# Two of four weight-block sums of a unit made by accumulating transfers, adaLN sums spread over the gate/up and down stages, h kept in blocks of halves

## The chip, the cores and the metric

The kernel runs on one core of a Trainium2 chip. The metric is the device time in microseconds of one execution; the time given for a kernel is the median of its runs. The program computes in fp32: a product of matrices is made as three matmuls of fp32r operands, each operand being split into a rounded part (hi) and the rest (lo).

## The reference

Batch 1, 512 tokens, D = 1024, two layers, each a token mixer and a SwiGLU FFN of width 2816. Every sub-layer is wrapped in RMS norms and in adaLN: shift, scale and gate come from a conditioning vector c.

```python
def ada_modulation(c, w, b):
    m = jax.nn.silu(c) @ w + b
    shift, scale, gate = jnp.split(m, 3, axis=-1)
...
for i in range(DEPTH):
    shift, scale, gate = ada_modulation(c, mix_ada_w[i], mix_ada_b[i])
    h = rms_norm(x, mix_pre_g[i]) * (1.0 + scale) + shift
    y = stick_breaking_mixer(...) if i % 2 == 0 else token_mixing_mixer(...)
    x = x + gate * rms_norm(y, mix_post_g[i])
    shift, scale, gate = ada_modulation(c, ffn_ada_w[i], ffn_ada_b[i])
    h = rms_norm(x, ffn_pre_g[i]) * (1.0 + scale) + shift
    y = (jax.nn.silu(h @ w_gate) * (h @ w_up)) @ w_down
    x = x + gate * rms_norm(y, ffn_post_g[i])
```

The token-mixing mixer (gMLP) makes u and v = gelu(h @ w_in), takes the layer norm of v, mixes it over 128 positions with w_s (sv), and projects u * sv with w_out.

## The kernel before, in words

The stages follow each other: attention of layer 0 (stage 0), its output projection, FFN 0 (stage 1: gate/up, then down), the gMLP (stage 2), its output projection, FFN 1 (stage 3: gate/up, then down). Tokens lie in four tiles of 128 (`tt`), the contraction in blocks of 128 (`k`), the FFN width in 22 units of 128 (`f`).

*Engines.* Matmuls are recorded at L71, in the order in which the program writes them; the engines work each through its own list in order. Weights arrive by SP's queue in 512 KB slabs (`raw`), ACT makes their hi (L94) and DVE their lo (L95). `wget` emits the loads and splits of slabs ahead of their use, three by default and one for the sevens. SP's queue is one list too, so an issue that waits for a buffer holds those behind it.

*Gate/up.* The first three units are plain products (`unit`, names `gu`). The other 19 of each FFN are `seven` (names `r`): gate and up over two halves of the tokens and two halves of the contraction are a 2x2 by 2x2 block product, made with seven products instead of eight (Winograd's form). A seven is 7 × 4 × 3 = 84 matmuls of 256 columns. It needs sums of the activation blocks (`S`, made once at the boundary by `sums`) and sums of the weight blocks, made by `blocks` for every unit: from the two slabs x (halves B11, B22) and y (B21, B12), `f13` = x + B12 (L152, both halves in one DVE instruction), then `f24` in two additions (L161, L162). x, f13, f24 and the half B21 are split into hi and lo. Buffers: two `raw` for x, two `raw2` for y, shared with the adaLN slabs, two `f13`, one `f24`.

*adaLN sums.* The first pair of vectors (stage 0's pre-norm) is made in the attention by `ada0_sum`. The others are ten vectors of 1024, each a sum over eight slabs of 512 KB (`rawada`, L290) scaled by silu(c), on DVE (L265), then summed over partitions by two pairs of matmuls with ones (`adaps`, L306 to L308), for which the sum is split first (`acch`, `accl`, L303). They are a generator `Bg`, and a call of `bg.step(n)` issues n slabs or closing steps. G of a stage is the gate and the post-norm's weight; A and B are the scale and shift of the next stage. `Bg(0)` runs in the attention and stage 0's projection; `Bg(1)` (G, A, B, 24 slabs) in FFN 0's down projection, two per `k`; `Bg(2)` (24 slabs) in the gMLP while v is made, three per `k`; `Bg(3)` (G, 8 slabs) in FFN 1's down projection.

*Projections.* `out_proj` adds over `k` into eight banks (four token tiles, two halves). While adaLN steps run it lends the banks of one tile to `adaps`, keeps that tile's first part in `yp`, and adds the two parts at the end (L476). The last four `k` are the tail, token tile by token tile, so that `boundary` of a tile (norm, gate, residual, norm, transposes `tp`, split into `hTh`, `hTl`) runs beside the matmuls of the next ones. `hT` is kept as four pairs of tiles, each for two `k` and all 512 tokens; `boundary` splits a transposed bank in two halves (L374 to L379). All such tiles are slots of one pool, `s4`, with 27 buffers.

*gMLP.* Five u units of the first token half run in FFN 0's boundaries; then their second half, v in two column halves, u units 5 to 7 as matmuls of 512 columns, and `mix` (sv). The layer norm of v runs on DVE and ACT beside u units 5 to 7.

Of the kernel before, what the change touches and what calls it, by code (L numbers as in the profile page):

```python
# [13 lines left out]
P = 128  # L14
T = 512
# [11 lines left out]
def trunk(ctx: ExitStack, tc: tile.TileContext, A: dict, out: bass.AP):  # L27
# [5 lines left out]
    adas = ctx.enter_context(tc.tile_pool(name="adas", bufs=2))  # L33
    npool = ctx.enter_context(tc.tile_pool(name="npool", bufs=2))
    small = ctx.enter_context(tc.tile_pool(name="small", bufs=4))
    s4 = ctx.enter_context(tc.tile_pool(name="s4", bufs=27))
# [68 lines left out]
    def wload():  # L105

        src, a, b, _ = stream[len(raws)]
        if src is None:
            raws.append(None)
            return  # L110
        raw = wraw.tile([P, a, b], F32, tag="raw", name=nm("raw"))
        load(raw[:], src)
        raws.append(raw)

    def wemit():
# [4 lines left out]
        if src is None:  # L120
            got.append(blocks(*key[1:]))
            return
# [13 lines left out]
    def blocks(src):  # L136
# [5 lines left out]
        xr = wraw.tile([P, KD, P], F32, tag="raw", name=nm("rawb"))  # L142
        yr = fwork["raw"].tile([P, KD, P], F32, tag="raw2", name=nm("rawb"))
        for e, t in enumerate((xr, yr)):
            load(t[:], A[src[0]][src[1:] + (e,)])
# [4 lines left out]
        split(b21[0][:], b21[1][:], yr[:, 0:4, :])  # L150
        f13 = fp.tile([P, KD, P], F32, tag="f13", name=nm("f13"))
        dve.tensor_tensor(  # L152
            f13[:].rearrange("p (a k) f -> p a (k f)", a=2),
            xr[:].rearrange("p (a k) f -> p a (k f)", a=2),
            yr[:, 4:8, :].rearrange("p (a k) f -> p a (k f)", a=1).to_broadcast([P, 2, 512]),
            ALU.add,
        )
# [4 lines left out]
        dve.tensor_tensor(f24[:, 4:8, :], f24[:, 0:4, :], yr[:, 0:4, :], ALU.add)  # L162
# [40 lines left out]
    for l in range(2):  # L203
# [3 lines left out]
        for f in range(NH, KF):  # L207
            stream.append((None, 0, 0, ("blocks", ("wgu", l, f))))
# [59 lines left out]

    class Bg:
# [5 lines left out]
        def __init__(self, s):  # L275
            self.s = s
            self.parts = [("G", s, 2)]
            if s < 3:
                self.parts += [("A", s + 1, 1), ("B", s + 1, 0)]
            self.gen = self.run()  # L280

        def run(self):
            for name, s, part in self.parts:
                acc = slot(F32, name, 1, D)[:, 0, :]
                setattr(self, name, acc)
# [7 lines left out]
            for name, s, part in self.parts:  # L293
                acc = getattr(self, name)
# [47 lines left out]
    def boundary(s, tt, y, bg, xin, hT, S, tag):  # L342
# [4 lines left out]
        for hf, c in enumerate(halves):  # L347
# [3 lines left out]
            dve.tensor_tensor(t[:, c], y[hf][:], bg.G[:, c], ALU.mult)  # L351
# [13 lines left out]
        dve.tensor_tensor(t[:], x[:], bg.A[:], ALU.mult)  # L365
        dve.reciprocal(r1[:], sd[:])
        dve.scalar_tensor_tensor(t[:], t[:], r1[:, 0:1], bg.B[:], ALU.mult, ALU.add)
        late = []
        for q in range(2):
# [4 lines left out]
            for k2 in range(2):  # L374
                th, tl = hT[q * 2 + k2]
                src = ps[:, k2 * 256 : (k2 + 1) * 256].rearrange("p (a b) -> p a b", a=2)
                split(
                    th[:, :, tt * P : (tt + 1) * P], tl[:, :, tt * P : (tt + 1) * P], src
                )  # L379
            a = ps[:].rearrange("p (a b) -> p a b", a=4)  # L380
            if S is not None and tt < 2:
# [38 lines left out]
    def out_proj(s, nk, get_act, wkey, J, bg, hT, nxt=(), pre=None, S=None, steps=0):  # L420
# [6 lines left out]
        mid = -(-8 * len(bg.parts) // steps) + 1 if steps else None  # L427
# [20 lines left out]
        for k in range(nk - J):  # L448
# [5 lines left out]
            bg.step(steps)  # L454
            if k + 1 == mid:
# [9 lines left out]
        if hT is not None and not hT:  # L465
            hT.extend(new_hT())
# [3 lines left out]
        for tt in range(NT):  # L470
# [7 lines left out]
            if tt < 2:  # L478
                boundary(s, tt, y[tt], bg, xin, hT, S, "p" if last == 0 else "b")
                xs[tt + 2] = x_load(tt + 2)  # L480
        evacs, late = [], []
        for n, tt in enumerate((2, 3)):
            if nxt:
                evacs.append(nxt[n]())
            late.append(boundary(s, tt, y[tt], bg, xin, hT, S, "p" if tt == 3 else "b"))
# [14 lines left out]
    bg = Bg(0)  # L500
# [46 lines left out]
    def ada0_sum(raws, n, nk):  # L547
        acc = adas.tile([P, 512], F32, tag="acch", name=nm("acc"))
# [67 lines left out]
    for b in range(1, 4):  # L616
# [11 lines left out]
        if b < 3:  # L628
            wload()
            acc = ada0_sum(an, 512, 2)  # L630
# [245 lines left out]
    class Ffn:  # L876
# [10 lines left out]
        def unit(self, f, lo, n, look=3):  # L887

            w = self.w(f, look)
            if n == T:  # L890
                g, u = bank("g"), bank("u")
                gp, up = g[:], u[:]
            else:
                g = bank("gu")
                gp, up = g[:, :n], g[:, n:]
            for pb, ww in ((gp, w[0]), (up, w[1])):
                for k in range(KD):
                    h, l = hTk(self.hT, k, lo, n)
# [16 lines left out]
        def seven(self, f):  # L915
# [4 lines left out]
            W = wget(("blocks", ("wgu", self.li, f)), 1)  # L920
            R1, R2, R3 = [bank(n)[:, :256] for n in ("r1", "r2", "r3")]
            S = {n: (lambda k, t=self.S[n]: (t[0][:, k, :], t[1][:, k, :])) for n in "1234"}
            S["A11"] = lambda k: hTk(self.hT, k, 0, 256)
            S["A12"] = lambda k: hTk(self.hT, k + 4, 0, 256)
            S["A22"] = lambda k: hTk(self.hT, k + 4, 256, 256)
# [65 lines left out]
    STEPS = 3  # L991
# [8 lines left out]
    def gmlp(bg, hT, nhT, nS, nxt):  # L1000
# [13 lines left out]
        def v_mm(vb, tt, k, w):  # L1014
            a, b = hTk(hT, k, tt * P, P)
# [100 lines left out]
    )  # L1116
    f0.run(
        Bg(1), hT2,
# [101 lines left out]
```

## Time and profile before

| | us |
|---|---|
| three runs | 1215.77, 1218.69, 1218.76 |
| median | 1218.69 |
| profiled execution | 1216.18 |
| its span, first to last instruction | 1214.4 |
| around the span | 1.8 |

In the profile, PE is the matrix engine, PEld its weight loads, DVE the vector engine, ACT the scalar engine, POOL the general one; SPq, POOLq and so on are their queues of issues. The page gives each engine's busy share, the span in 40 slices of 30.4 us (digits are tenths; PEclk is the clock granted to the matrix engine), the chain of work that ended last, groups of instructions by line and tile, and DMA issues with their time from issue to landing. "out<-in" are the program's names of tiles. Where matmuls follow closely their recorded durations overlap, so a rate is taken from a stretch and its count. A few records of matmuls can be missing.

### The profile page before, as it was taken

Reading aid. Unit: us, or ns where it says so; the run is one execution under the profiler, and the core shown is the slowest. Engines: PE = TensorE matmul, PEld = TensorE weight load, DVE = VectorE, ACT = ScalarE, POOL = GpSimd, SP = SyncE. Lnnn points to the kernel's source line nnn. Section 1 sums busy time; section 2 is a strip of 40 time slices with the busy share of each in tenths; the row PEclk is TensorE's granted clock in tenths of the full one; section 3 lists DMA queues with packets and bytes.
Section 4 is the critical chain, followed back from the end, with each engine's and each line's share of the span. In section 5 each row is a group of like instructions: output and inputs, shape, how many; then the busy total and the mean of one; then the engine's idle time right before and its main releaser. Section 6 shows DMA issues by size and latency. Waiting matters only on the chain.

```text
span 1214.4 us, 18534 instructions
## 1 busy us (share of the span) xinstructions
PE 1179.5 (97%) x7336; PEld 1032.4 (85%) x7336; DVE 888.3 (73%) x1247; ACT 627.4 (52%) x1097; POOL 18.0 (1%) x30
## 2 busy tenths in 40 slices
PE   7898999999999999999999999899999999999998
PEld 4777778787899999998877898688999999998886
DVE  5878887766699888878763867785998888778224
ACT  6455766786555555556232542444655555555212
POOL 0100000000000000000000010000000000000000
PEclk9999999999999999999999999889999999999999
DMA  9666351120443333336883468734323333356311
GB/s 334 229 202 206 115 157 55 36 86 8 140 149 105 105 105 104 105 105 210 277 290 108 152 214 279 226 119 139 123 88 105 105 105 105 109 197 201 118 52 69
DMA packets 48634, 174.14 MB, mean 143 GB/s; under 512 B 5658, under 2 KB 5786, under 8 KB 48548
## 3 DMA queue, kind: packets, MB, share of 16 engines
q1 hardware_dynamic: 46820, 166.67, 42.8%
q0 software_dynamic: 1728, 6.29, 1.4%
q8 instruction: 57, 0.93, 0.3%
q14 instruction: 29, 0.24, 0.1%
HBM read 164.56 MB, written 8.39 MB: 142 GB/s over the span
## 4 chain that ended last, share of the span: by engine, by line
PE 71%; DMA 11%; DVE 11%; ACT 3%; issue 3%; SPq 0%; DVEq 0%; ACTq 0%
PE r L71 31%; PE y L71 20%; DMA rawada<-in_ada 6%; PE pqk L71 4%; PE gu L71 3%; PE av L71 2%; PE v L71 2%; DVE wl L95 2%; PE z3h L71 2%; PE z0h L71 2%; DMA raw<-in_wdown 2%; DVE A L265 1%; DMA raw<-in_win_v 1%; PE u L71 1%; ACT wh L94 1%
## 5 line engine op out<-in xcount | busy, mean ns | idle before, releaser
L71 PE MATMUL y<-wh,as 128*128 128x512 f32 x832 | 265.3, 397 | 0.0
L94 ACT ACTIVATE wh<-raw 128x1024 fp32r<-128x1024 f32 x112 | 118.4, 1059 | 208.8 <-PE y L71 105.9
L95 DVE TENSOR_TENSOR wl<-raw,wh 128x1024 fp32r<-128x1024 f32 x112 | 136.4, 1221 | 101.9 <-ACT wh L94 101.6
L71 PEld LDWEIGHTS y<-wh,as 128*128 128x128 f32 x832 | 157.3, 189 | 37.5 <-ACT B L310 0.4
L71 PE MATMUL r<-Sh,wh 128*128 128x256 f32 x608 | 170.1, 280 | 0.2 <-ACT e L938 0.2
L71 PE MATMUL r<-Sh,wl 128*128 128x256 f32 x608 | 170.3, 280 | 0.0
L71 PE MATMUL r<-Sl,wh 128*128 128x256 f32 x608 | 170.0, 280 | 0.0
L71 PE MATMUL y<-wl,as 128*128 128x512 f32 x416 | 165.1, 397 | 0.0
L95 DVE TENSOR_TENSOR wl<-f,wh 128x1024 fp32r<-128x1024 f32 x76 | 92.9, 1222 | 53.6 <-ACT wh L94 53.6
L94 ACT ACTIVATE wh<-f 128x1024 fp32r<-128x1024 f32 x76 | 80.7, 1061 | 76.1 <-PE r L71 72.3
L71 PEld LDWEIGHTS r<-Sh,wh 128*128 128x128 f32 x608 | 114.6, 189 | 0.4 <-ACT e L938 0.4
L71 PEld LDWEIGHTS r<-Sl,wh 128*128 128x128 f32 x608 | 114.5, 188 | 0.0
L71 PEld LDWEIGHTS r<-Sh,wl 128*128 128x128 f32 x608 | 114.5, 188 | 0.0
L71 PEld LDWEIGHTS y<-wl,as 128*128 128x128 f32 x416 | 78.7, 189 | 17.9
L71 PE MATMUL r<-hTh,wh 128*128 128x256 f32 x304 | 89.0, 293 | 0.0
L71 PE MATMUL r<-hTl,wh 128*128 128x256 f32 x304 | 84.9, 279 | 0.0
L71 PE MATMUL r<-hTh,wl 128*128 128x256 f32 x304 | 79.5, 280 | 0.0
L71 PEld LDWEIGHTS r<-hTh,wh 128*128 128x128 f32 x304 | 57.2, 188 | 5.4 <-DVE gu L948 0.7
L71 PE MATMUL r<-hTh,b 128*128 128x256 f32 x304 | 60.6, 282 | 0.0
L94 ACT ACTIVATE wh<-rawb 128x1024 fp32r<-128x1024 f32 x38 | 40.4, 1062 | 35.0 <-PE r L71 30.9
L71 PEld LDWEIGHTS r<-hTl,wh 128*128 128x128 f32 x304 | 57.3, 189 | 0.0
L95 DVE TENSOR_TENSOR wl<-rawb,wh 128x1024 fp32r<-128x1024 f32 x38 | 46.6, 1225 | 12.0 <-ACT wh L94 12.0
(245 smaller groups left out, 2664.1 us busy)
## 6 DMA issues: line engine op xcount, KB each, us to landing
rawada<-in_ada SPq DMA_DIRECT2D x80, 512.0 KB, 4.3
rawb<-in_wgu SPq DMA_DIRECT2D x76, 512.0 KB, 4.3
raw<-in_wdown SPq DMA_DIRECT2D x44, 512.0 KB, 4.2
raw<-in_wqk SPq DMA_DIRECT2D x16, 512.0 KB, 3.7
ada<-in_ada0p SPq DMA_DIRECT2D x12, 512.0 KB, 9.3
raw<-in_wgu SPq DMA_DIRECT2D x12, 512.0 KB, 4.4
xd<-x POOLq DMA_DIRECT2D x12, 512.0 KB, 2.9
x<-xd SPq DMA_DIRECT2D x12, 512.0 KB, 4.5
```

Source lines behind the costliest of these rows:

```text
L71: b = nc.tensor.matmul(o, l, r, start=start, stop=stop, skip_group_check=True)
L94: act.activation(hi, src, AF.Copy)
L95: dve.tensor_tensor(lo, src, hi.bitcast(F32), ALU.subtract)
L265: dve.scalar_tensor_tensor(acc, w, sc[:, kk : kk + 1], acc, ALU.mult, ALU.add)
```

## The change

- `blocks`: the second weight array `wy` holds, beside B21, the half B12 twice. f13 is loaded with x a second time, and POOL's queue adds the 512 KB `wy[4:12]` onto it by a transfer with `accum_op=add`; the DVE addition L152 is gone. y is loaded as 256 KB instead of 512. The transfers of a block are emitted one block ahead (`block_loads`). f24 is made as before.
- adaLN sums: G of stage 1 and A of boundary 1 in FFN 0's sevens (one or two steps a unit); B of boundary 1 and G of stage 2, then A and B of boundary 2, in FFN 0's down projection; in the gMLP what is left of the generator, one step per `k`; G of stage 3 in FFN 1's sevens, and no steps in FFN 1's down projection, so that there is no `yp` there. `adas` has one buffer of each kind instead of two, and the attention's sums take the two kinds in turn.
- hT: tiles of four `k` and 256 tokens, allocated as `boundary` comes to them; one split per transposed bank instead of two. Every matmul over `hT` has at most 256 columns; u units 5 to 7 take two where they took one. `s4` has 28 buffers.

The diff, without empty lines and most of its context; left out are the attention's and v's calls with the new names:

```diff
@@ -30,10 +30,10 @@
-    adas = ctx.enter_context(tc.tile_pool(name="adas", bufs=2))
+    adas = ctx.enter_context(tc.tile_pool(name="adas", bufs=1))
...
-    s4 = ctx.enter_context(tc.tile_pool(name="s4", bufs=27))
+    s4 = ctx.enter_context(tc.tile_pool(name="s4", bufs=28))
@@ -104,9 +104,9 @@
-        src, a, b, _ = stream[len(raws)]
+        src, a, b, key = stream[len(raws)]
...
-            raws.append(None)
+            raws.append(block_loads(key[1]))
@@ -118,7 +118,9 @@
         if src is None:
-            got.append(blocks(*key[1:]))
+            if len(raws) == n + 1 < len(stream) and stream[n + 1][0] is None:
+                wload()
+            got.append(blocks(*raws[n]))
             return
@@ -133,33 +135,35 @@
-    def blocks(src):
-        xr = wraw.tile([P, KD, P], F32, tag="raw", name=nm("rawb"))
-        yr = fwork["raw"].tile([P, KD, P], F32, tag="raw2", name=nm("rawb"))
-        for e, t in enumerate((xr, yr)):
-            load(t[:], A[src[0]][src[1:] + (e,)])
+    def block_loads(idx):
+        fp = fwork["pool"]
+        x = wraw.tile([P, KD, P], F32, tag="raw", name=nm("rawx"))
+        y = fwork["raw"].tile([P, 4, P], F32, tag="raw2", name=nm("rawy"))
+        f13 = fp.tile([P, KD, P], F32, tag="f13", name=nm("f13"))
+        wx, wy = A["wx"][idx], A["wy"][idx]
+        load(x[:], wx)
+        load(f13[:], wx)
+        load(y[:], wy[:, 0:4, :])
+        nc.gpsimd.dma_start(out=f13[:], in_=wy[:, 4:12, :], accum_op=ALU.add)
+        return x, y, f13
+    def blocks(xr, yr, f13):
...
-        split(b21[0][:], b21[1][:], yr[:, 0:4, :])
-        f13 = fp.tile([P, KD, P], F32, tag="f13", name=nm("f13"))
-        dve.tensor_tensor(
-            f13[:].rearrange("p (a k) f -> p a (k f)", a=2),
-            xr[:].rearrange("p (a k) f -> p a (k f)", a=2),
-            yr[:, 4:8, :].rearrange("p (a k) f -> p a (k f)", a=1).to_broadcast([P, 2, 512]),
-            ALU.add,
-        )
+        split(b21[0][:], b21[1][:], yr[:])
...
-        dve.tensor_tensor(f24[:, 4:8, :], f24[:, 0:4, :], yr[:, 0:4, :], ALU.add)
+        dve.tensor_tensor(f24[:, 4:8, :], f24[:, 0:4, :], yr[:], ALU.add)
@@ -205,7 +209,7 @@
-            stream.append((None, 0, 0, ("blocks", ("wgu", l, f))))
+            stream.append((None, 0, 0, ("blocks", (l, f - NH))))
@@ -266,23 +270,25 @@
         )
+    ada = {}
     class Bg:
-        def __init__(self, s):
-            self.s = s
-            self.parts = [("G", s, 2)]
-            if s < 3:
-                self.parts += [("A", s + 1, 1), ("B", s + 1, 0)]
+        def __init__(self, *parts):
+            self.parts = [
+                (n, int(s), int(s) + (n != "G"), {"G": 2, "A": 1, "B": 0}[n]) for n, s in parts
+            ]
             self.gen = self.run()
         def run(self):
-            for name, s, part in self.parts:
+            for name, at, s, part in self.parts:
                 acc = slot(F32, name, 1, D)[:, 0, :]
-                setattr(self, name, acc)
+                ada[name, at] = acc
                 nc.gpsimd.memset(acc, 0.0)
@@ -290,8 +296,8 @@
-            for name, s, part in self.parts:
-                acc = getattr(self, name)
+            for name, at, s, part in self.parts:
+                acc = ada[name, at]
@@ -339,7 +345,13 @@
-    def boundary(s, tt, y, bg, xin, hT, S, tag):
+    def hB(hT, k, lo, n):
+        h, l = hT[lo // 256, k // 4]
+        lo %= 256
+        return h[:, k % 4, lo : lo + n], l[:, k % 4, lo : lo + n]
+    def boundary(s, tt, y, xin, hT, S, tag):
@@ -362,22 +374,21 @@
         sd, r1 = rms(sx[:])
-        dve.tensor_tensor(t[:], x[:], bg.A[:], ALU.mult)
+        dve.tensor_tensor(t[:], x[:], ada["A", s], ALU.mult)
         dve.reciprocal(r1[:], sd[:])
-        dve.scalar_tensor_tensor(t[:], t[:], r1[:, 0:1], bg.B[:], ALU.mult, ALU.add)
+        dve.scalar_tensor_tensor(t[:], t[:], r1[:, 0:1], ada["B", s], ALU.mult, ALU.add)
         late = []
...
                 transpose(ps[:, k * P : (k + 1) * P], t[:, kk * P : (kk + 1) * P])
-            for k2 in range(2):
-                th, tl = hT[q * 2 + k2]
-                src = ps[:, k2 * 256 : (k2 + 1) * 256].rearrange("p (a b) -> p a b", a=2)
-                split(
-                    th[:, :, tt * P : (tt + 1) * P], tl[:, :, tt * P : (tt + 1) * P], src
-                )
             a = ps[:].rearrange("p (a b) -> p a b", a=4)
+            if tt % 2 == 0:
+                hT[tt // 2, q] = (slot(F32R, "hTh", 4, 256), slot(F32R, "hTl", 4, 256))
+            c = slice(tt % 2 * P, (tt % 2 + 1) * P)
+            th, tl = hT[tt // 2, q]
+            split(th[:, :, c], tl[:, :, c], a)
             if S is not None and tt < 2:
@@ -417,14 +428,14 @@
-    def out_proj(s, nk, get_act, wkey, J, bg, hT, nxt=(), pre=None, S=None, steps=0):
+    def out_proj(s, nk, get_act, wkey, J, bg, hT, nxt=(), pre=None, S=None, steps=0, bg2=None):
...
-        mid = -(-8 * len(bg.parts) // steps) + 1 if steps else None
+        mid = min(nk - J, -(-8 * len(bg.parts) // steps) + 1) if steps else None
@@ -452,6 +463,8 @@
+            if bg2 is not None and mid is not None and k >= mid:
+                bg2.step(2)
@@ -476,13 +487,13 @@
-                boundary(s, tt, y[tt], bg, xin, hT, S, "p" if last == 0 else "b")
+                boundary(s, tt, y[tt], xin, hT, S, "p" if last == 0 else "b")
...
-            late.append(boundary(s, tt, y[tt], bg, xin, hT, S, "p" if tt == 3 else "b"))
+            late.append(boundary(s, tt, y[tt], xin, hT, S, "p" if tt == 3 else "b"))
@@ -544,8 +555,8 @@
-    def ada0_sum(raws, n, nk):
-        acc = adas.tile([P, 512], F32, tag="acch", name=nm("acc"))
+    def ada0_sum(raws, n, nk, tag="acch"):
+        acc = adas.tile([P, 512], F32, tag=tag, name=nm("acc"))
@@ -627,7 +638,7 @@
-            acc = ada0_sum(an, 512, 2)
+            acc = ada0_sum(an, 512, 2, ("acch", "accl")[b % 2])
@@ -887,15 +898,11 @@
-            if n == T:
-                g, u = bank("g"), bank("u")
-                gp, up = g[:], u[:]
-            else:
-                g = bank("gu")
-                gp, up = g[:, :n], g[:, n:]
+            g = bank("gu")
+            gp, up = g[:, :n], g[:, n:]
...
-                    h, l = hTk(self.hT, k, lo, n)
+                    h, l = hB(self.hT, k, lo, n)
@@ -917,12 +924,12 @@
-            W = wget(("blocks", ("wgu", self.li, f)), 1)
+            W = wget(("blocks", (self.li, f - NH)), 1)
...
-            S["A11"] = lambda k: hTk(self.hT, k, 0, 256)
-            S["A12"] = lambda k: hTk(self.hT, k + 4, 0, 256)
-            S["A22"] = lambda k: hTk(self.hT, k + 4, 256, 256)
+            S["A11"] = lambda k: hB(self.hT, k, 0, 256)
+            S["A12"] = lambda k: hB(self.hT, k + 4, 0, 256)
+            S["A22"] = lambda k: hB(self.hT, k + 4, 256, 256)
@@ -959,14 +966,16 @@
             return rest
-        def run(self, bg, nhT, nxt, nS=None):
+        def run(self, bg0, bg, bg2, steps, nhT, nxt, nS=None):
             for f in range(NH):
...
                 self.seven(f)()
+                bg0.step(1 + (f % 3 == 0))
+            bg0.step(99)
             out_proj(
                 self.s, KF, lambda k: act_split(self.act[k // 2][:, k % 2, :]),
-                lambda k: ("wdown", self.li, k), 4, bg, nhT, nxt, None, nS, 2,
+                lambda k: ("wdown", self.li, k), 4, bg, nhT, nxt, None, nS, steps, bg2,
             )
@@ -975,8 +984,12 @@
-            h, l = hTk(hT, k, lo, n)
-            mm3(ub[:, :n], w[0][:, k, :], w[1][:, k, :], h, l, k == 0, k == KD - 1)
+            for c in range(0, n, 256):
+                h, l = hB(hT, k, lo + c, 256)
+                mm3(
+                    ub[:, c : c + 256], w[0][:, k, :], w[1][:, k, :], h, l,
+                    k + c == 0, k == KD - 1,
+                )
@@ -988,7 +1001,7 @@
-    STEPS = 3
+    STEPS = 1
@@ -1106,20 +1119,20 @@
-    hT1, hT2, hT3 = [], [], []
+    hT1, hT2, hT3 = {}, {}, {}
...
-    hT1.extend(new_hT())
...
+    bg2 = Bg("A2", "B2")
...
-        Bg(1), hT2,
+        Bg("G1", "A1"), Bg("B1", "G2"), bg2, 2, hT2,
...
-    gmlp(Bg(2), hT2, hT3, S3, f1.first())
-    f1.run(Bg(3), None, ())
+    gmlp(bg2, hT2, hT3, S3, f1.first())
+    f1.run(Bg("G3"), bg2, None, 0, None, ())
@@ -1130,11 +1143,12 @@
-    def blocks(a, b, n):
-        x = np.concatenate([a[:, :, :4], b[:, :, 4:]], 2)
-        y = np.concatenate([a[:, :, 4:], b[:, :, :4]], 2)
-        return np.concatenate([np.stack([a[:n], b[:n]], 1), np.stack([x[n:], y[n:]], 1)])
+    def blocks(a, b):
+        return (
+            np.concatenate([a[:, :, :4], b[:, :, 4:]], 2),
+            np.concatenate([a[:, :, 4:], b[:, :, :4], b[:, :, :4]], 2),
+        )
@@ -1150,12 +1164,9 @@
-    a["wgu"] = np.stack(
-        [
-            blocks(fout(i["ffn_w_gate"][l]), fout(i["ffn_w_up"][l]), 3)
-            for l in range(2)
-        ]
-    )
+    gu = [(fout(i["ffn_w_gate"][l]), fout(i["ffn_w_up"][l])) for l in range(2)]
+    a["wgu"] = np.stack([np.stack([g[:3], u[:3]], 1) for g, u in gu])
+    a["wx"], a["wy"] = [np.stack(t) for t in zip(*[blocks(g[3:], u[3:]) for g, u in gu])]
```

More of the change, by code (lines that the diff above doesn't have):

```diff
@@ L350, in boundary @@
                 sd, r2 = rms(sq[1][:], sq[0][:])
-            dve.tensor_tensor(t[:, c], y[hf][:], bg.G[:, c], ALU.mult)
+            dve.tensor_tensor(t[:, c], y[hf][:], ada["G", s][:, c], ALU.mult)
         dve.reciprocal(r2[:], sd[:])
@@ L464, in out_proj @@
         ]
-        if hT is not None and not hT:
-            hT.extend(new_hT())
         sqrt_table()
@@ L497, in sqrt_table @@
             nc.scalar.preload_act_table_set("sqrt_and_others")
-    bg = Bg(0)
+    bg = Bg("G0", "A0", "B0")
     b1 = consts.tile([P, KD], F32, name="b1")
@@ L1014, in v_mm @@
         def v_mm(vb, tt, k, w):
-            a, b = hTk(hT, k, tt * P, P)
+            a, b = hB(hT, k, tt * P, P)
             mm3(vb[tt][:], a, b, w[0][:, k % 2, :], w[1][:, k % 2, :], k == 0, k == KD - 1)
```

## The prediction

> **What bounds the kernel now.** I read the page first: busy shares, the slices and the chain of work that ended last.
>
> ```profile
> PE 1179.5 (97%) x7336; PEld 1032.4 (85%) x7336; DVE 888.3 (73%) x1247; ACT 627.4 (52%) x1097; POOL 18.0 (1%) x30
> PEclk9999999999999999999999999889999999999999
> DMA  9666351120443333336883468734323333356311
> PE 71%; DMA 11%; DVE 11%; ACT 3%; issue 3%; SPq 0%; DVEq 0%; ACTq 0%
> 374.26 178.50 PE r L71 x1487
> 893.01 190.01 PE r L71 x1584
> 1113.50 94.94 PE y L71 x408
> ```
>
> TensorE (PE) is the bound: 97% busy. The three long rows of the chain are pure PE: a 256-column matmul of the sevens takes 178.50/1487 = 0.120 us, a 512-column one of a down projection 94.94/408 = 0.233 us. A seven is 84 matmuls, so 84 × 0.120 = 10.1 us. There, time off other engines buys nothing, and what counts is whether something new outlasts 10 us. The granted clock is short in two slices only, the 26th and 27th (30.4 us each: 759 to 820 us), the gMLP. So I cut that stretch up.
>
> ```profile
> 750.00:760.00 10.00, 10.00 (x44) 7.80 (x42) 6.52 (x7) 0.58 (x1) 0.00 (x0) 1.00 0.88 299
> 760.00:770.00 10.00, 5.25 (x13) 3.52 (x13) 6.55 (x8) 2.59 (x5) 0.00 (x0) 0.72 0.86 278
> 770.00:780.00 10.00, 10.00 (x42) 7.99 (x41) 9.14 (x14) 6.19 (x8) 0.00 (x0) 0.94 0.55 160
> 780.00:790.00 10.00, 9.95 (x44) 7.79 (x42) 8.45 (x10) 5.58 (x6) 0.00 (x0) 1.00 0.74 231
> 790.00:800.00 10.00, 7.51 (x48) 6.88 (x49) 10.00 (x14) 8.36 (x12) 0.00 (x0) 0.92 0.54 188
> 800.00:810.00 10.00, 10.00 (x42) 8.94 (x42) 8.75 (x13) 2.52 (x4) 0.00 (x0) 0.56 0.46 159
> ```
>
> The columns are stretch, length, busy time of PE, weight load, DVE, ACT and POOL, then granted clock, DMA share and GB/s. PE is idle 4.75 us in the second row and 2.49 us in the fifth, and behind both holes it runs on at a lower clock: 0.72, and 0.56 in the last row. What it waits for stands in the timeline and in the view of the tile adaps (the small matmuls that end each adaLN sum):
>
> ```profile
> 758.16 1.29 DVE L265 SCALAR_TENSOR_TENSOR A<-rawada,sc,A 128x1024 f32<-128x1024 f32 x1 [0.59 <-DMA rawada<-in_ada]
> 763.02 1.15 ACT L94 ACTIVATE acch<-A 128x512 fp32r<-128x512 f32 x2 [2.06 <-DVE A L265]
> 763.71 0.50 PE L71 MATMUL adaps<-acch,cr 128*128 128x512 f32 x1 [3.60 <-ACT acch L94]
> 766.94 0.79 PE L71 MATMUL adaps<-accl,cr 128*128 128x512 f32 x1 [1.15 <-DVE accl L95]
> 790.98 0.50 PE L71 MATMUL adaps<-acch,cr 128*128 128x512 f32 x1 [1.02 <-ACT acch L94]
> 794.84 0.33 PE L71 MATMUL sv<-wsh,vnh 128*128 128x128 f32 x1 [0.79 <-ACT vnh L94]
> 796.78 0.33 PE L71 MATMUL sv<-wsh,vnl 128*128 128x128 f32 x1 [0.72 <-DVE vnl L95]
> ```
>
> The chain is transfer of a rawada slab, sum on DVE (L265), split on ACT, adaps on PE. PE runs in order, so the v matmuls stand behind adaps. The later sv holes wait for the layer norm, on a DVE that is full (10.00 of 10).
>
> **What the change removes here.** In the order in which the changed program's instructions stand, the gMLP holds no L265 and no rawada load: the three sums that stood there (24 slabs) are made in f0's down projection, and at most the closing adaps of two of them remain, far behind their sums. Idle: 4.75 + 0.05 + 2.49 = 7.3 us. Clock, as (1 − granted) × busy: 0.28×5.25 + 0.06×10 + 0.08×7.51 + 0.44×10 = 7.1 us. Together 14.4 us. Of the idle time 1.5 us (0.79 + 0.72) is the layer norm's; its DVE no longer shares with these sums, and the last three u units, 72 matmuls of 512 columns before (72 × 0.233 = 16.8 us of PE), stand between the last v and the first sv. I leave 1.0 us for it: **−13.4 us** (ends: 0, if another wait takes over, and −14.4).
>
> **Where the sums go.** All 80 remain.
>
> ```profile
> 556.78 3.50 DMA raw<-in_wdown
> ...
> 580.00:600.00 20.00, 8.95 (x8) 1.00 0.85 275
> 600.00:620.00 20.00, 8.92 (x7) 1.00 0.85 281
> 640.00:700.00 60.00, 0.00 (x0) 1.00 0.38 130
> 700.00:800.00 100.00, 30.72 (x24) 0.96 0.71 233
> 1085.00:1110.00 25.00, 7.69 (x6) 1.00 0.70 240
> L265 DVE SCALAR_TENSOR_TENSOR A<-rawada,sc,A x24: 1275/1284/1287, 101.5 to 761.7; 128x1024 f32<-128x1024 f32 x24
> ```
>
> (A row of the chain; then stretch, length, busy time and count of L265 alone, clock, DMA share, GB/s.) f0's down projection gets 32 sums instead of 24, f0's sevens 16, f1's sevens 8, f1's down none. In f0 down DMA is 85% busy at two sums and one wdown slab per step (24 matmuls, 5.6 us), and PE is whole: the next sixteen sums simply continue that load into the stretch which now has 0.38. At 20 us per 7.5 sums, 2.7 us each, 16 sums from about 620 us end at 663 us, when tail tile 0 (18 × 5.6 + 5.6 us after 556.8 us) ends too; three tail tiles, 16.8 us of PE, cover what is late. Past 3.7 us per sum ((663 + 16.8 − 620)/16) that cover is gone, and the last wdown slabs and the first boundary are late next. Also adas has one buffer instead of two; B1 and G2 end in series. I take **+1 us** (ends 0 and +10).
>
> **The sevens.** Each loses one DVE addition and gains a second load of x into f13, an accumulating transfer of 512 KB from POOL's queue, and half of the y load disappears (38 blocks).
>
> ```profile
> 380.00:540.00 160.00, 160.00 (x1338) 158.02 (x1337) 128.90 (x175) 85.44 (x144) 0.00 (x0) 1.00 0.37 108
> L152 DVE TENSOR_TENSOR f<-rawb,rawb 128x1024 f32<-128x1024 f32 x15 | 18.3, 1220 | 0.0
> L94 ACT ACTIVATE wh<-f 128x1024 fp32r<-128x1024 f32 x76 | 80.7, 1061 | 76.1 <-PE r L71 72.3
> L95 DVE TENSOR_TENSOR wl<-f,wh 128x1024 fp32r<-128x1024 f32 x76 | 92.9, 1222 | 53.6 <-ACT wh L94 53.6
> q1 hardware_dynamic: 46820, 166.67, 42.8%
> q0 software_dynamic: 1728, 6.29, 1.4%
> rawb<-in_wgu SPq DMA_DIRECT2D x76, 512.0 KB, 4.3
> xd<-x POOLq DMA_DIRECT2D x12, 512.0 KB, 2.9
> x<-xd SPq DMA_DIRECT2D x12, 512.0 KB, 4.5
> ```
>
> DVE: 128.90/16 = 8.06 us per seven, less 1.22, plus 1.28 × 16/12 = 1.71 where sums run: 8.6 of 10 us. That fits; the 38 × 1.22 = 46 us saved were hidden behind PE and give nothing by themselves. DMA: 281 GB/s at a share of 0.85 makes 0.524 MB cost 0.85 × 0.524/0.281 = 1.6 us of all 16 engines. Per seven: x, f13 and half a y 2.5 × 1.6 = 4.0; ada slabs 1.33 × 1.6 = 2.1 in the first 12 blocks of f0 and 8 of f1; the accumulation 1.6 c, where c is its weight in plain loads. No row shows an accumulating transfer. Nearest rows: POOL's plain write is no dearer than a load (q0: 1.4%/6.29 MB against 42.8%/166.67 MB, 0.22 against 0.26% per MB), so c = 0.9 below; it reads the weight, reads f13 and writes f13, three passages, so c = 3 above. A round trip, xd and back, is two plain transfers: I take **c = 2**. Then 4.0 + 2.1 + 3.2 = 9.3 us with sums and 7.2 without, under 10.1: **0 us**, with little to spare. In time: a load 4.3 us and a round trip 2.9 + 4.5 = 7.4 us make 11.7 us from f13's issue; with two f13 buffers each is turned over in two blocks, 20.2 us, of which its split takes 1.06 + 1.22, so some 17 us are left. Behind f13's load in SP's queue, y, the next sums and the next x wait; behind the accumulation on POOL only the next one. End at c = 3: 10.9 us with sums, 20 × 0.8 = +16 us; at c = 0.9, 0.
>
> The Trainium skill ("Collectives: The Full Stack", Why ReduceScatter is half of AllGather) has an add in the DMA engines cost its two source reads, a measured ratio of 62.28/32.35 = 1.93; an estimate by it is c = 1.9 and 9.2 us, under PE's time as well. No run here has shown it.
>
> **Boundaries, and the rest.** One split of 128x512 replaces two of 128x256, and L152 leaves the end of the first boundary:
>
> ```profile
> L94 ACT ACTIVATE hTh<-tp 128x256 fp32r<-128x256 f32 x16 | 5.9, 382 | 4.2 <-PE tp L79 2.2 <-DVE hTl L95 1.8
> L94 ACT ACTIVATE b<-rawb 128x512 fp32r<-128x512 f32 x2 | 1.2, 624 | 0.0
> 351.01 1.23 DVE f L152
> 352.23 0.34 DVE hTl L95
> ```
>
> 4 × 0.382 − 2 × 0.624 = 0.3 us of ACT per token tile, and L152's 1.23 us stood ahead of the last hTl, for which gu waits. I take **−1.0 us** (ends 0 and −3). In f1 down, with no steps, token tile 0's sum waits for the last Silu behind 7 matmuls (1.6 us) instead of 18 (4.2 us): **+1 us** (0 to 2.6). Three u units become 256-column pairs: 72 × (2 × 0.120 − 0.233) = **+0.5 us**. Removing f1 down's sums and the yp copies gives nothing, PE being whole there.
>
> **Sum:** −13.4 + 1 + 0 − 1.0 + 1 + 0.5 = −11.9 us. The profiled execution took 1216.18 us (span 1214.4): 1204.3. The runs shown are 1215.77 to 1218.76 with median 1218.69, so the profiled one lies at the low end; half of that difference, 1.2 us, added: **1205 us**, its own range 1199 to 1212.
>
> **Rivals.**
> *A, slower: the accumulating transfer sets the pace of the sevens.* Place: t13's split waits for f13, and PE for t13. For it: no row of its cost, 9.3 of 10.1 us already at c = 2, two buffers, one POOL queue. Against: 17 us of turnover against 11.7, and 18 blocks without sums in which arrears are made good. It eats the gain from c = 2.7 (20 × (6.1 + 1.6c − 10.1) = 6 us) to 2.9 (12 us) on; at c = 3 it costs 16 us, 1221; at c = 4, 20 × 2.4 + 18 × 0.3 = 53 us: 1258. I price it at 1235, between the two.
> A rule that speaks for A: the Trainium skill ("SBUF — State Buffer", SBUF: two separate sides, the "DVE blocks DMA" trap) says that transfers from GpSimd's queue starve while DVE runs its two-port fast modes. The sevens' DVE rows are tensor_tensor at 1220 ns per 1024 elements, without a faster kind among them, so by that rule nothing happens here; no run shows it yet.
> *B: the stall moves into f0's down projection.* For it 32 sums at 0.85 of DMA and the serial ends on one buffer; against it the 16.8 us of tail. At +8 us instead of +1: 1212.
> *C: the gMLP keeps its second hole.* The layer norm on DVE still holds sv, and the low clock follows: only the first hole returns, 4.75 + 1.47 + 0.6 = 6.8 us, 1212; if a late win_v slab takes the first hole over too, 1218. For it: sv waits even now beside adaps. Against: DVE loses 10 us of sums there.
> *That the change doesn't take the sums out of the gMLP* is excluded by the order of instructions.
>
> **Chances.** Forecast 0.42, A 0.32, B 0.12, C 0.14. What a measurement can tell from no change is 0.3%, 3.7 us. Faster: 0.42 + 0.12 + 0.09 of C; within: 0.05 of C and 0.02 of A; slower: 0.30 of A. So 0.63, 0.07 and 0.30. The range must take in most of A: 1196 to 1244; the likeliest's own stands above.
>
> **What would show it.** In the gMLP, stretches of 10 us with PE at 10.00 and clock 1.00, and no adaps waiting for ACT; left-over idle at sv speaks for C. In the sevens, still 0.120 us per matmul with a DMA share of 0.7 to 0.95; a share of 1 with PE idle before r, t13's split waiting for f13, or f13's accumulation landing later than some 12 us show A. In f0's down, PE waiting before y or at the first transposes shows B. The forecast is wrong if the chain's r rows break up, or if the clock falls below 1.00 in the sevens.

## The result and the profile after

The change made the kernel slower by a little: 1224.4 us median (1220.66 to 1229.3, 9 runs) against 1218.23 (1211.68 to 1221.66, 9 runs), ratio 1.0061, 95% interval 1.0035 to 1.0088. The forecast was 1205 us.

The page of the changed kernel, the lines that answer to those of before; the last two rows are issues with KB each and the median time from issue to landing:

```profile
PE 1176.3 (96%) x7408; PEld 1031.6 (85%) x7408; DVE 846.6 (69%) x1183; ACT 621.3 (51%) x1071; POOL 51.4 (4%) x68
PEclk9999999999999999999999999999999999999999
DMA  8666341121648868776888453314477777635311
q1 hardware_dynamic: 52292, 176.64, 43.2%
q0 software_dynamic: 7200, 26.22, 11.2%
PE 66%; DVE 14%; DMA 11%; issue 4%; ACT 4%; DVEq 0%; SPq 0%; ACTq 0%
PE y L71 24%; PE r L71 19%; DMA rawada<-in_ada 7%; PE v L71 5%; PE pqk L71 4%; DVE wl L95 4%; PE u L71 3%; PE av L71 2%; PE z3h L71 2%; PE z0h L71 2%; DMA raw<-in_wgu 1%; PE gu L71 1%; ACT wh L94 1%; PE tp L79 1%; PE z2h L71 1%
rawada<-in_ada SPq DMA_DIRECT2D x80, 512.0 KB, 4.3
f<-in_wy POOLq DMA_DIRECT2D x38, 512.0 KB, 5.9
```

The clock digits are whole now, and the chain's long rows of r have broken up: r had 31% of it and has 19%. Stretches of the same kernel show both sides (columns as before; the third row is 102 us long):

```profile
380.00:430.00 50.00, 46.65 (x380) 45.00 (x379) 37.57 (x50) 23.99 (x42) 3.46 (x5) 1.00 0.80 233
430.00:480.00 50.00, 44.97 (x371) 43.75 (x370) 39.79 (x55) 24.31 (x40) 5.32 (x6) 1.00 0.79 219
578.00:680.00 102.00, 102.00 (x441) 82.30 (x440) 76.66 (x77) 34.33 (x45) 0.95 (x1) 1.00 0.83 277
680.00:800.00 120.00, 119.49 (x735) 105.81 (x733) 71.54 (x91) 59.23 (x97) 2.70 (x5) 1.00 0.38 123
900.00:950.00 50.00, 46.46 (x379) 44.90 (x378) 38.10 (x50) 23.92 (x41) 3.46 (x4) 1.00 0.81 231
1000.00:1050.00 50.00, 50.00 (x419) 49.27 (x418) 35.53 (x51) 26.98 (x45) 4.33 (x5) 1.00 0.70 180
```

The gMLP (680 to 800) has lost its holes, and FFN 0's down projection (578 to 680) is whole in spite of 32 sums. The sevens, whole before, now have holes, in FFN 0 and in the first part of FFN 1: where adaLN slabs are summed. From 1000 us on, with the accumulating transfers still running and the sums done, PE is whole again.

Starts of matmuls in the profiled execution give the stages: sevens from the first to the last r, the gMLP from the first u to the last sv, FFN 1's down projection from the last r to the last y.

| us | sevens FFN 0 | sevens FFN 1 | gMLP | first gu to first r, FFN 0 | last r of FFN 0 to first u | FFN 1 down | span |
|---|---|---|---|---|---|---|---|
| before | 192.8 | 192.8 | 128.8 | 38.2 | 127.3 | 122.3 | 1214.4 |
| after | 209.7 | 200.6 | 113.0 | 36.1 | 125.6 | 121.3 | 1219.5 |

That is +24.7 us in the sevens, −15.8 in the gMLP, −2.1, −1.7 and −1.0 in the next three, +1.0 in the rest: +5.1 us in these two executions, +6.2 in the medians.

Not all of the 24.7 us is waiting. PE is idle for 10.8 us of FFN 0's sevens and 4.7 us of FFN 1's (before: 0.2 and 0.0). Twelve closing matmuls of the sums (adaps), 0.23 us each, now stand in the sevens, eight and four: 2.8 us that left the down projections and the gMLP, where four fewer stand in each. And from 480 to 490 us, behind a hole of 1.82 us, the granted clock was 0.83, which costs 1.7 us. The other some 5 us are matmuls at the edges of 22 holes, whose recorded time of 0.28 to 0.39 us is not overlapped there.

What PE waits for leads back to DVE's list. From the view of waits of the changed kernel, 370 to 570 us (engine, line and what it waits for: us in total, times, longest):

```profile
DVE G L269 <- DMA rawada<-in_ada: 13.6, 7, 2.8
DVE A L269 <- DMA rawada<-in_ada: 12.3, 6, 3.5
PE r L71 <- DVE gu L955: 5.5, 5, 1.8
PE r L71 <- ACT e L951: 2.5, 4, 1.0
PE r L71 <- ACT e L949: 1.1, 3, 0.7
```

One place of it, in the timeline of the changed kernel (DVE and PE first, then SP's queue, then ACT):

```profile
403.75 1.28 DVE L269 SCALAR_TENSOR_TENSOR G<-rawada,sc,G 128x1024 f32<-128x1024 f32 x1 [2.08 <-DMA rawada<-in_ada]
...
409.20 1.28 DVE L269 SCALAR_TENSOR_TENSOR G<-rawada,sc,G 128x1024 f32<-128x1024 f32 x1 [0.16 <-DMA rawada<-in_ada]
410.40 0.42 DVE L953 TENSOR_TENSOR gu<-r,e 128x256 f32<-128x256 f32 x1
410.74 1.22 DVE L95 TENSOR_TENSOR wl<-rawx,wh 128x1024 fp32r<-128x1024 f32 x1
411.87 0.41 DVE L955 TENSOR_TENSOR gu<-e,r 128x256 f32<-128x256 f32 x1
412.34 0.39 PE L71 MATMUL r<-hTh,wh 128*128 128x256 f32 x1 [1.50 <-DVE gu L955]
...
416.18 1.29 DVE L269 SCALAR_TENSOR_TENSOR G<-rawada,sc,G 128x1024 f32<-128x1024 f32 x1 [2.77 <-DMA rawada<-in_ada]
...
405.06 0.33 SPq L88 DMA_DIRECT2D rawada<-in_ada  x1
409.10 0.33 SPq L88 DMA_DIRECT2D rawy<-in_wy  x1
410.51 0.33 SPq L88 DMA_DIRECT2D rawada<-in_ada  x1
...
419.57 0.42 ACT L959 ACTIVATE gu<-gu 128x256 f32<-128x256 f32 x1 [2.20 <-DVE gu L947]
419.90 0.36 ACT L951 ACTIVATE e<-r 128x256 f32<-128x256 f32 x1
```

The sum of 403.75 has waited 2.08 us for its slab. When it ends it frees a buffer (403.75 + 1.28), and the next slab is issued, at 405.06. DVE works on without a break until 409.04 and then waits 0.16 us for that slab; behind this second sum stand the two evacuations L953 and L955 (instructions that take PE's results out of their banks). PE's last product of the block adds onto the bank that L955 reads, and starts when L955 ends, 1.50 us late. The slab after that is issued at 410.51, when the sum of 409.20 has freed a buffer (409.20 + 1.28), and keeps DVE idle for 2.77 us. y shares the two buffers with the slabs.

About half of PE's idle time in FFN 0 is a wait for ACT (e, L949 and L951). In the place shown it goes back to the same list: after the sum of 416.18 DVE makes gu (L947) late, ACT's L959 waits 2.20 us for it, e (L951) stands behind L959, and the matmul that needs e starts at 420.31, 0.56 us late.

### The profile page after: what moved, and what is told of

It is laid out like the page before. It is cut to its first block, busy times and chain, and to the rows that moved or that the text cites. A ratio compares the mean times of both kernels' runs of the same rounds, so it can differ in the third digit from the quotient of the medians.

```text
span 1219.5 us, 18827 instructions
## 1 busy us (share of the span) xinstructions
PE 1176.3 (96%) x7408; PEld 1031.6 (85%) x7408; DVE 846.6 (69%) x1183; ACT 621.3 (51%) x1071; POOL 51.4 (4%) x68
## 3 DMA queue, kind: packets, MB, share of 16 engines
q1 hardware_dynamic: 52292, 176.64, 43.2%
q0 software_dynamic: 7200, 26.22, 11.2%
## 4 chain that ended last, share of the span: by engine, by line
PE 66%; DVE 14%; DMA 11%; issue 4%; ACT 4%; DVEq 0%; SPq 0%; ACTq 0%
PE y L71 24%; PE r L71 19%; DMA rawada<-in_ada 7%; PE v L71 5%; PE pqk L71 4%; DVE wl L95 4%; PE u L71 3%; PE av L71 2%; PE z3h L71 2%; PE z0h L71 2%; DMA raw<-in_wgu 1%; PE gu L71 1%; ACT wh L94 1%; PE tp L79 1%; PE z2h L71 1%
## 5 line engine op out<-in xcount | busy, mean ns | idle before, releaser
L269 DVE SCALAR_TENSOR_TENSOR G<-rawada,sc,G 128x1024 f32<-128x1024 f32 x32 | 41.1, 1283 | 41.3 <-DMA rawada<-in_ada 39.2
L152 POOL DMA_DIRECT2D f<-in_wy x38 | 33.2, 881 | 645.6 <-ACT wh L94 262.6
```

Of the source, the lines that this page charges most:

```text
L152: nc.gpsimd.dma_start(out=f13[:], in_=wy[:, 4:12, :], accum_op=ALU.add)
L269: dve.scalar_tensor_tensor(acc, w, sc[:, kk : kk + 1], acc, ALU.mult, ALU.add)
```

## The experiments

Three theories were to be told apart. Theory 1: the sum on DVE's list waits for its slab, and the evacuations behind it hold PE. Theory 2: the accumulating transfers set the pace. Theory 3: the sum's 1.28 us on DVE suffices to displace the evacuations. Each run has a profile and a median against the kernel before on the same chip. Times of stages are those of one profiled execution each; executions of one kernel on one chip differ by 3 to 10 us in all.

### One half of the change alone

**acc_only**: accumulating transfers and h blocks, the sums where they stood before.

```diff
-        Bg("G1", "A1"), Bg("B1", "G2"), bg2, 2, hT2,
+        None, Bg("G1", "A1", "B1"), None, 2, hT2,
-    f1.run(Bg("G3"), bg2, None, 0, None, ())
+    f1.run(None, Bg("G3"), None, 2, None, ())
...
```

> The accumulating transfers and the h blocks stay; the adaLN sums stand where they stood before (24 in FFN 0's down, 24 in the gMLP, 8 in FFN 1's down), with two adas buffers. Measured from the first to the last r matmul, a sevens stage took 192.8 us in both FFNs before, and 209.7 and 200.6 us after the change; from the first u to the last sv matmul the gMLP took 128.8 and 113.0 us. Theory 1 (a sum in DVE's list waits for its slab, evacuations stand behind it, PE behind them): both sevens 193 +-1, gMLP 127 to 130, profiled span 1212 to 1217. Theory 2 (accumulating transfers set the pace): both sevens above 198, span above 1222. Theory 3 (the sum's 1.28 us on DVE alone displaces the evacuations): as theory 1.

Sevens 193.3 and 192.7, gMLP 128.9, span 1217.6 us (0.6 over theory 1's band), ratio 1.0008 (0.9987 to 1.0030). The accumulating transfers alone do not slow the sevens: theory 2 falls as the whole cause. They bring nothing there either, since the additions taken off DVE were hidden.

**dve_add**: the sums where the change puts them, f13 added on DVE.

```diff
-        load(f13[:], wx)
-        load(y[:], wy[:, 0:4, :])
-        nc.gpsimd.dma_start(out=f13[:], in_=wy[:, 4:12, :], accum_op=ALU.add)
+        load(y[:], wy[:, 0:8, :])
...
+        dve.tensor_tensor(f13[:]..., xr[:]..., yr[:, 4:8, :]..., ALU.add)
```

> The opposite half: f13 is added on DVE again and y is one 512 KB slab, no accumulating transfer; the adaLN sums stand where the change puts them. Theory 1: sevens 205 to 215 and 198 to 204 us, span 1215 to 1226. Theory 2: sevens 193 +-1 in both, gMLP 113, span 1194 to 1199. Theory 3: slower than the change, since DVE has 1.22 us more per block: sevens above 212 and 202.

Sevens 201.1 and 198.4, gMLP 113.0, span 1213.7, ratio 0.9965 (0.9946 to 0.9985). The stall is there without any accumulating transfer, but smaller than the change's 209.7 and 200.6, by 8.6 and 2.2 us. FFN 0 is 3.9 us and the span 1.3 us under theory 1's band: the accumulating transfers make the stall worse, which no theory had by itself. One way is seen: DVE waits for slabs 6.2 us from 370 to 570 us, against 25.9 in the change. Theory 3 asked for more stall with a busier DVE, and there was less.

### The sum without its slab

**no_slab**: the sums of the sevens keep their places and read a constant.

```diff
+                    if self.dry:
+                        ada_stt(acc, oneb[:].to_broadcast([P, D]), k)
+                        yield
+                        continue
...
```

> As the change, but the 24 sums in the sevens read a constant column and load no slab (G and A of stage 1 and G of stage 3 are left out of the computation so far as their weights go); each sum keeps its place and its 1.28 us on DVE. Theory 1: sevens 193 to 195 us in both, span 1194 to 1200. Theory 3: sevens still 205 to 210 and 198 to 201. Theory 2: transfers fall from about 9.3 to 7.2 us per block, so it allows 193 to 195 too, and falls or stands by the other runs.

Sevens 194.9 and 195.0, gMLP 113.2, span 1199.2, ratio 0.9890 (0.9867 to 0.9912). The waits of DVE in 370 to 570 us, all of them, and two stretches:

```profile
DVE wl L95 <- ACT wh L94: 24.9, 28, 1.7
DVE gu L959 <- PE r L71: 12.6, 12, 3.2
DVE act L969 <- ACT gu L966: 1.0, 1, 1.0
```

```profile
380.00:430.00 50.00, 50.00 (x421) 49.48 (x421) 39.46 (x54) 27.51 (x47) 5.29 (x6) 1.00 0.70 184
430.00:480.00 50.00, 50.00 (x422) 49.64 (x421) 44.45 (x58) 27.30 (x46) 4.37 (x5) 1.00 0.68 182
```

No wait of DVE for a transfer is left, and PE is whole with the sums still on DVE: theory 3 falls. Some 2 us a stage remain over 192.8: the closing matmuls, and 0.7 and 0.8 us of idle PE.

### Slabs loaded earlier

**ahead**: y in a small buffer of its own, slabs two sums ahead, still one or two steps a block.

```diff
+                if not self.slabs:
+                    self.fetch()
+                    self.fetch()
...
-                    ada_stt(acc, raw[:], k)
+                    ada_stt(acc, self.slabs.pop(0)[:], k)
+                    self.fetch()
...
-        y = fwork["raw"].tile([P, 4, P], F32, tag="raw2", name=nm("rawy"))
+        y = fwork["raw"].tile([P, 4, P], F32, tag="rawy", bufs=1, name=nm("rawy"))
```

> As the change, but y has a buffer of its own (one of 256 KB) and the two larger ones are for slabs alone, loaded two sums ahead; the first sum of a stage comes one step later; the scratch tile of the squares is bf16 to make room. Every transfer, sum and place on DVE stays. Theory 1: sevens 193 to 197 us in both, gMLP 113, span 1195 to 1202, faster than both kernels. Theory 2 and theory 3: sevens still 205 to 210 and 198 to 201, span 1215 to 1221.

A miss for theory 1: 203.3 and 200.5, span 1216.8, ratio 1.0008 (0.9988 to 1.0028). Emitted ahead is not issued ahead. The scheduler, which sets the order of each engine's list, drew sums and slab loads together, as the timeline of this kernel's SP queue shows:

```profile
457.57 0.33 SPq L88 DMA_DIRECT2D f<-in_wx  x1
458.77 9.12 SPq L88 DMA_DIRECT2D rawada<-in_ada  x3
469.02 0.33 SPq L88 DMA_DIRECT2D rawx<-in_wx  x1
```

Three slab loads in a row, the later ones each waiting for a sum, hold the next block's x for over 9 us; the sum at 466.24 waited 2.09 us for its slab, and PE had the largest hole of its sevens there (2.8 us). But in all DVE waited for slabs only 4.8 us from 370 to 570 us, against 25.9 in the change, and 10.5 and 7.7 us of the stall stayed. So the slab's wait in DVE's list is not the whole of it in this kernel. Sums drawn together behind a short wait, and x and f13 late behind slabs in SP's queue, are what else its timeline shows; the runs do not separate the two.

**one_step**: one adaLN step a block, each slab still loaded in its own step.

```diff
-                self.seven(f)()
-                bg0.step(1 + (f % 3 == 0))
+                rest = self.seven(f)
+                tail = f - (KF - 3) if self.li == 0 else -1
+                if tail >= 0:
+                    bg0.step(1)
+                rest()
+                bg0.step((2, 2, 1)[tail] if tail >= 0 else 1)
```

> As the change, but with one adaLN step a block instead of one or two (the closing steps of G1 and A1 in the last three blocks); a slab is still loaded in the step that sums it. Sevens so far: 209.7 and 200.6 us with slabs, 194.9 and 195.0 without. If the late slab alone sets the wait, a third of the steps in a pair of which the second waits for a whole load is gone, and the single ones remain: 200 to 206 and 197 to 200 us, span 1208 to 1216. If the bursts of two are all of it: 194 to 197 in both, span 1198 to 1203.

201.8 and 199.6, span 1214.7: at most a part of the stall goes with the pairs of steps. This profile lies at the lowest of its run's times; the ratio is 1.0040 (1.0019 to 1.0062), and against the change's 1.0061 (1.0035 to 1.0088) that is no clear gain.

**even_acc** and **even_dve**: one step a block and each slab one step ahead, in the two buffers shared with y; the second with f13 added on DVE.

```diff
+            self.fetch()
+            if self.early:
+                yield
...
+                    ada_stt(acc, self.slabs.pop(0)[:], k)
+                    self.fetch()
+                    yield
```

> As one_step, and each slab is loaded one step ahead of its sum, so that y and the slabs take the two shared buffers in turn and every load has a block's time (10 us) to land. Theory 1 (late slab on DVE's list): sevens 193 to 197 us in both, gMLP 113, span 1196 to 1202, faster than both kernels. If the load on the transfers (0.80 of all engines) itself matters, as the 8.6 us between the change and dve_add in FFN 0 (209.7 against 201.1) hint: 198 to 204 and 197 to 200.

> As even_acc, but f13 is added on DVE and there is no accumulating transfer, so DVE has 9.3 of 10.1 us of work in a block with a sum. Theory 1: sevens 193 to 197 us, span 1196 to 1202. If DVE's work itself (theory 3) shows once it is nearly full: 197 to 203 in the blocks with sums, FFN 0 by twice as much over 193 as FFN 1, since it has 16 sums against 8.

even_acc missed: 206.7 and 201.6, ratio 1.0081 (1.0060 to 1.0102), above both of its bands. even_dve: 198.6 and 197.7, span 1205.9, ratio 0.9943 (0.9927 to 0.9959), above theory 1's bands and within the other's 197 to 203, though FFN 0 is not twice as far over 193 as FFN 1. DVE still waited for slabs, 5.1 us from 370 to 570 us. In even_acc the buffers crossed over. Its timeline, SP and DVE:

```profile
405.86 0.33 SPq L88 DMA_DIRECT2D rawy<-in_wy  x1
409.90 0.33 SPq L88 DMA_DIRECT2D rawada<-in_ada  x1
...
404.55 1.28 DVE L269 SCALAR_TENSOR_TENSOR G<-rawada,sc,G 128x1024 f32<-128x1024 f32 x1 [2.12 <-DMA rawada<-in_ada]
...
409.14 0.69 DVE L166 TENSOR_TENSOR f<-f,rawy 128x512 f32<-128x512 f32 x1
...
416.03 1.29 DVE L269 SCALAR_TENSOR_TENSOR G<-rawada,sc,G 128x1024 f32<-128x1024 f32 x1 [3.26 <-DMA rawada<-in_ada]
```

y is issued when the sum ends (404.55 + 1.28 = 405.83), the slab when f24 has read y (409.14 + 0.69 = 409.83): each waits for the other's buffer, and the slab comes late again.

### Slabs in time

**own_acc** and **own_dve**: as the two before, with buffers that y and the sevens' slabs do not share, and with sum and load held in their places.

```diff
+                b = nc.sync.dma_start(out=raw[:], in_=A["ada"][self.todo.pop(0)])
+                if last_y[0] is not None:
+                    order(b, last_y[0])
...
+                    b = ada_stt(acc, self.slabs.pop(0)[:], k)
+                    if self.early and last_v[0] is not None:
+                        order(b, last_v[0])
```

> As even_acc (one sum a block, accumulating transfers), but y has one buffer of its own, the two shared ones are for slabs alone, the sum is held behind the block's last product on DVE (act) and its next slab behind y in SP's queue; the scratch tile of the squares is bf16. In even_acc a slab took y's old buffer and y the slab's, so a slab was loaded only when f24 had read y, some 5 us ahead of its sum. Theory 1 (the slab's arrival): sevens 193.5 to 196 us in both FFNs, no wait of DVE for rawada, span 1196 to 1201. If the accumulating transfers' load on the engines matters beyond that: 198 or more in FFN 0, with DVE waiting for y or t13 waiting for f13.

> As even_dve (one sum a block, f13 added on DVE), with a buffer for the sevens' slabs of their own, one f13 buffer instead of two, and the sum and the slab's load held in place as in own_acc. Theory 1: sevens 193.5 to 196 us in both, span 1196 to 1201, like own_acc. If DVE's 9.3 of 10.1 us matter: 197 or more in FFN 0, half of the excess in FFN 1, with PE waiting for gu on DVE and DVE waiting for nothing.

own_dve: sevens 193.8 and 194.2, in theory 1's band, span 1201.5, 1201.43 us median, ratio 0.9883 (0.9858 to 0.9908). It is the fastest kernel that computes everything, 1.2% faster than before. Its stretches:

```profile
380.00:480.00 100.00, 100.00 (x836) 98.67 (x835) 94.72 (x121) 54.51 (x91) 0.00 (x0) 1.00 0.49 157
900.00:1000.00 100.00, 100.00 (x835) 98.61 (x834) 91.94 (x119) 54.87 (x92) 0.00 (x0) 1.00 0.44 142
```

DVE is 95% busy and PE is whole: work that fits does no harm where nothing in the list waits. With no_slab, that shows theory 1 without accumulating transfers. own_acc: 196.7 and 198.6, span 1205.5, 1205.54 us median, ratio 0.9914 (0.9889 to 0.9938), above theory 1's bands; FFN 0 is under the 198 of the other. DVE waits for no slab there, but its f13 was late, most of all in one place, in the timeline of ACT, DVE and PE:

```profile
899.05 1.06 ACT L94 ACTIVATE wh<-f 128x1024 fp32r<-128x1024 f32 x1 [1.31 <-DMA f<-in_wy]
...
899.04 0.69 DVE L165 TENSOR_TENSOR f<-f,rawx 128x512 f32<-128x512 f32 x1 [3.08 <-issue]
...
902.31 0.58 PE L71 MATMUL r<-hTh,wh 128*128 128x256 f32 x1 [2.88 <-DVE gu L971]
```

L165 starts as ACT is released by the accumulation, and the evacuation behind it (L971) is late. So beside slabs that are in time the accumulating transfers cost 2.9 and 4.4 us in the two stages (196.7 − 193.8, 198.6 − 194.2). In FFN 1 that one hole is nearly all of it: 2.88 us, and the granted clock was 0.83 from 900 to 910 us, which costs another 1.3.

**acc_twice**: acc_only with every accumulation issued twice.

```diff
         nc.gpsimd.dma_start(out=f13[:], in_=wy[:, 4:12, :], accum_op=ALU.add)
+        nc.gpsimd.dma_start(out=f13[:], in_=wy[:, 4:12, :], accum_op=ALU.add)
```

> As acc_only, but every accumulating transfer is issued twice (B12 enters f13 two times, so that part of gate and up is changed). acc_only had sevens of 193.3 and 192.7 us. By the change's own queue rows one accumulation costs 2.0 plain loads, 3.1 us of all 16 engines: x, f13 and half a y 3.9 and two accumulations 6.3 make 10.2 us of 10.1. If that price is right and the transfers can set the pace: sevens 195 to 206, DMA share 0.95 or more in them. If an accumulation is cheaper than its rows say, or its latency is covered: 193 +-1 and a share below 0.9.

243.2 and 239.2, span 1313.1, ratio 1.0794 (1.0760 to 1.0827): far outside both bands. The share was 0.79, not 0.95. The second accumulation waits for the first, in the waits of 380 to 560 us of this kernel:

```profile
POOL f L153 <- DMA f<-in_wy: 76.4, 14, 6.6
PE r L71 <- DVE gu L956: 20.0, 9, 4.2
```

A load of f13 (6.9 us in that window) and two accumulations (6.1 us each) make 19.1 us on one buffer, with the wait for its release and the split to come; two buffers allow one block in half of the whole, and a block took 243.2/19 = 12.8 us. With a fifth of the engines' time free, their load does not set the pace; the turnover of the f13 buffers is the reading that fits. A part of the longer stages is the clock, granted at 0.92 and 0.94 in them.

## Why the prediction was wrong, step by step

- **gMLP, −13.4 us**: the mechanism was right; it measured −15.8, beyond the end of −14.4. Idle and low clock both went; sv no longer waits, so the 1.0 us held back for the layer norm was not needed. The clock's term came from six rows; over the whole stage before, PE was busy 121.51 us at a clock of 0.93, which is 8.5 us and not 7.1. And four closing matmuls left the stage (0.9 us).
- **Sums in FFN 0's down, +1**: right in kind, −1.7; 32 sums at a share of 0.83 cost PE nothing, and B did not come.
- **Boundaries −1.0, FFN 1's down +1, u units +0.5**: −2.1 for the stretch of FFN 0's units, −1.0 for FFN 1's down, and the u units lie inside the gMLP's gain. All small. The sum moved the adaLN sums between stages and not their closing matmuls: that is why FFN 1's down came out shorter (four adaps and two y, 1.4 us, stand in the sevens now).
- **Weight of an accumulation, c = 2**: right. From the page of the changed kernel, q0 has 11.2% of 1219.5 us, less 17.0 us for the twelve xd (1.4% of 1214.4): 119.6/38 = 3.15 us each; a load of q1 0.432 × 1219.5 × 0.524/176.64 = 1.56 us. c = 2.0. The Trainium skill's ratio of 1.93 ("Collectives: The Full Stack", Why ReduceScatter is half of AllGather) agrees with it.
- **The sevens, 0 us**: this step failed; they cost +24.7 us. "8.6 of 10 us. That fits" counted work and not order. The work does fit (no_slab, own_dve). What the step left out is that the sum brings a wait into DVE's list, between evacuations that PE needs within a product's time of 1.4 us (12 × 0.120), and that the slab's load cannot be early, because it needs a buffer that y or the last sum still holds. Behind f13's load the text named the queue on SP, but for the sum it named nobody. By the runs, of the 24.7 us some 20 go with the slabs (no_slab keeps 4.3 = 2.1 + 2.2). With the accumulating transfers in place, slabs in time and one sum a block save 15.0 of the 24.7 (own_acc keeps 9.7 = 3.9 + 5.8); with f13 added on DVE, late slabs leave 13.9 us (dve_add) and slabs in time 2.4 (own_dve). So the late slab is the larger part, and the accumulating transfers make it worse. The medians, each against the kernel before on its chip, say the same: +6.2 us for the change and −6.0 for dve_add, −9.9 for own_acc and −14.0 for own_dve, so the accumulating transfers cost 12 us beside late slabs and 4 beside slabs in time.
- **Rival A** had the place and the sign and another cause: alone, in acc_only, t13's split and f13 did not set the pace. Beside slabs the transfers do cost time, but own_acc shows it at one late f13 and not as a pace. Its prices took 20 blocks with sums, "8 of f1"; at one or two steps a unit the eight sums of FFN 1 take six blocks, so there are 18, and c = 3 would have cost 14 us instead of 16.
- **The range** held 1224.4, on A's side, by luck: for a reason that was not A's. Of the signs named, two came: the chain's r rows broke up, and the clock fell below 1.00 in the sevens, in one stretch of 10 us.

The last 1.0 and 1.4 us in own_dve's stages are no wait: PE is busy for 193.85 of 193.9 and 194.2 of 194.2 us, with the closing matmuls among its work. Open stays how the accumulating transfers and the late slabs make each other worse, beyond the waits shown. Buffers of their own for y and the slabs were tried with the scheduler's order only in ahead, with one or two sums a block; one sum a block with separate buffers and no held order was not tried.

## What to carry to other kernels

An operation moved onto an engine with room to spare is priced by its wait and by what stands behind it in that engine's list, not only by its duration: 24 sums of 1.28 us that fitted cost some 20 us with slabs that came late, and next to nothing with slabs in time and no accumulating transfers. Give such an operation data that landed a block earlier. In own_dve that took a buffer of its own and a place held in both lists (the two came together, so neither is shown to do it alone); emitting the load earlier in the program was not enough. Where work moves between stages, move its closing steps in the sum too. And an addition that is hidden gained nothing here by going to a transfer (acc_only), which brings a latency and a buffer's turnover of its own.

## What was not expected of the hardware

An accumulating transfer of 512 KB took 5.9 us from issue to landing beside 2.9 us for POOL's plain one before, and twice a load's time of the engines; two of them on one tile, the second held until the first had landed, took 6.1 us each and left the engines at a share of 0.79 while PE was idle for 33 of the 243 us of FFN 0's sevens. The issue took POOL 0.86 to 0.89 us each time in the sevens, with DVE busy 75% of FFN 0's with tensor_tensor and scalar_tensor_tensor, so none was stretched by DVE's work. That is in line with the Trainium skill ("SBUF — State Buffer", SBUF: two separate sides), which has such transfers starve while DVE runs its two-port fast modes; the trace does not name DVE's mode.
